# Trainium2 kernel study: moving the DRAM crossings of an encoder kernel from the ACT and POOL queues to SP's queue

## The chip, the cores and the metric

The kernel runs on one core of one Trainium2 chip. The time is device microseconds (us) of one execution. Before the change, three runs gave 878.9, 880.5 and 880.49 us, so the median is 880.49 us.

Engines are named as the profile names them: PE does the matrix multiplications, DVE and ACT work on vectors, POOL and SP here mostly issue transfers. A DMA transfer is issued by an instruction in the queue of one engine. An engine runs its queue in order, so an instruction that waits holds up everything behind it in the same queue.

## The reference

Two layers over 256 tokens of width 1024, in float32. A layer has a token mixer and a gated MLP, each with a residual:

```python
def _token_mixer(xn, w_in, w_pool, pool_scale, w_a, w_b, w_o, rel_bias):
    B, S, _ = xn.shape
    u, q, k, v, g_pool, g_attn = jnp.split(xn @ w_in, SPLITS, axis=-1)
    ...
    for gi, (window, dilation) in enumerate(ATTN_GROUPS):
        ...
        o_g, lse_g = _dilated_group(q[:, :, hs], k[:, :, hs], v[:, :, hs], bias, window, dilation)
    ...
    wts = jax.nn.softmax(jnp.stack(lses, axis=0), axis=0)
    attn = jnp.einsum('gbsh,gbshd->bshd', wts, jnp.stack(outs, axis=0).astype(jnp.float32))
    ...
    merged = jax.nn.sigmoid(g_pool) * (pool_out @ w_a) + jax.nn.sigmoid(g_attn) * (attn_out @ w_b)
    return merged @ w_o

def _conv_ffn(xn, w_up, conv_w, conv_b, w_down):
    a, gval = jnp.split(xn @ w_up, 2, axis=-1)
    a = lax.conv_general_dilated(...) + conv_b
    return (jax.nn.gelu(a) * gval) @ w_down

def reference(x, w_in, ...):
    h = x
    for layer in range(DEPTH):
        h = h + _token_mixer(_rmsnorm(h, norm1[layer]), ...)
        h = h + _conv_ffn(_rmsnorm(h, norm2[layer]), ...)
    return _rmsnorm(h, norm_f)
```

## The kernel before

**Weights.** All weights stream from DRAM once, through the class `Weights`. A load brings 1 MB into one of three `raw` buffers (L145, issued by SP; a load of the q and k weights is two issues of 512 KB). To keep the precision of float32, each load is split into two pieces, and each piece into a high part `wh` (a cast on ACT, L208) and a low part `wl` (a subtraction on DVE, L210). There are five buffers for split pieces, and PE multiplies with `wh` and `wl` in turn. `W.get()` hands out the next piece and splits the pieces that are due after it. `W.loads_behind` maps the number of a load to an instruction: that load is put into SP's queue only after this instruction (`issue_after`). It sets an order in the queue; it is not a wait for data.

**Crossings.** Some products come out of PE with tokens on the partitions and are needed with channels on the partitions. `cross` (L732) does this in three steps: two DVE transposes of 32 x 32 blocks, a write of 512 KB to a DRAM tile (L741), and four reads of 128 KB from it into a quarter of the partitions each (L746). The reads wait until the write has landed. Every layer has sixteen crossings:

- six for q and k (`n` = 0 to 5 in the loop that calls `by_tokens`, tiles "crossing" into `k` and `qk_rows`). The write is issued by ACT (`there=nc.scalar`), the reads by POOL;
- four for the probabilities, one for each head of the first group (`start_turn(hh)`, tile "turning" into `turned_p`), write on ACT, reads on POOL;
- six in the MLP (`to_z`, tile "crossing" into `zg` and `zga`), write on SP, reads on POOL.

**The stage around them.** From the q and k projections to the gates, PE, ACT and DVE run in the order in which the source is written (`manual_schedule`). The matmuls of weight pieces are `t_ps` (L692). After each piece, `step()` runs what the table `steps` has for that place: `parts` splits k and q of the first head group, `scores(hh)` (matmuls `s_ps`, L1055 and L1061, then the softmax), `start_turn(hh)`, `turn(hh)` (the high part `pth` on ACT, L1100, and the low part `ptl` on DVE, L1101) and `weigh(hh)` (matmuls `o_ps`, L1110 and L1114). `scores(0)` multiplies with k of crossing 3. `turn(0)` and `weigh(0)` come after the piece at place 28 and 29. In ACT's order the cast of the first piece of load 27 stands ahead of `pth` of `turn(0)`, and in DVE's order the subtraction of that piece stands ahead of `ptl`.

Elsewhere, the MLP among it, a scheduler orders the instructions by their dependences and by the `issue_after` that the source gives. Loads are counted within the kernel: in the first layer, loads 10 to 22 bring the weights of q and k (and one of them those inside the pooling mixer), loads 23 to 26 w_a, 27 to 30 those of the first gate, 31 to 36 those of the second gate and w_b, 37 to 40 w_o, and from load 41 on those of the MLP. `first_up[l]` has the number of the first load of w_up, 41 in the first layer; this load goes to a buffer of its own and is called by hand at place 39 of `steps`.

**Before, on SP,** nothing of the q, k and probability crossings stands in the queue. The loads follow one another as raw buffers come free. In the MLP the write of a crossing stands between loads.

Of the kernel before, what the change touches and what calls it, by code (L numbers as in the profile page):

```python
# [23 lines left out]
HPG = 4  # L24
# [73 lines left out]
class Weights:  # L98
# [8 lines left out]
    def __init__(self, tc, pool, idle):  # L107
        self.tc, self.nc, self.pool, self.idle = tc, tc.nc, pool, idle
        self.loads, self.pieces = [], []
        self.n_loaded, self.n_split, self.n_got = 0, 0, 0  # L110
        self.look = self.LOOK
        self.raw, self.split = {}, {}
        self.live = set()
        self.behind, self.later = (), []
        self.last = [None, None]
        self.loads_behind = {}
        self.n_scaled, self.gains = 0, None

    def add(self, src, shape, cuts, tag=None):
# [129 lines left out]
def encoder(ctx, tc, x, w_in, w_pool, pool_scale, w_a, w_b, w_o, norm1, norm2, w_up, conv_w,  # L249
            conv_b, w_down, rel_bias, norm_f, onehot, edges, out):  # L250
    nc = tc.nc
# [9 lines left out]
    W = Weights(tc, wpool, big)  # L261
# [32 lines left out]
    first_up = []  # L294
    for l in range(DEPTH):
# [37 lines left out]
        for f in range(4, NF, 2):  # L333
            if f in HALF_GROUPS:
                n, j = HALF_GROUPS[f]
# [343 lines left out]
    def run(gen):  # L679
        for _ in gen:  # L680
            pass

    def v_tile():
        return acc.tile([P, 512], F32, tag="acc", name="v_ps")
# [12 lines left out]
    def by_tokens(x2, n, at_once=1, then=None, ps=None, begin=0, end=None,  # L697
                  ahead=None):


        if ps is None:
            ps = [mmp.tile([P, 512], F32, tag="mm", name="t_ps") for _ in range(2)]
        for i0 in range(begin, n if end is None else end, at_once):
            if ahead:
                next(ahead)
            held = [W.get() for _ in range(at_once)]
            for t in range(2):
                for i, piece in enumerate(held, i0):
                    v_sum(ps[t], x2, t, i, piece, n - 1)
            for i, _ in held:  # L710
                W.free(i)
            if then:
                then()
        return ps

    def to_chunks(rows, y, z, parts):

        turned = nc.vector.transpose(out=y.rearrange("p q c j -> p c q j"), in_=rows)  # L720
        d = dram.tile([P, 4, P], F32, tag="turned", bufs=4, name="turned")
        nc.sync.dma_start(out=d, in_=y.rearrange("p q c j -> p q (c j)"))
        for q in range(4):
            there = nc.sync.dma_start(
                out=z[32 * q : 32 * q + 32].rearrange("p a c j -> p a (c j)"),
                in_=d[:, q].rearrange("(a i) x -> i a x", a=4),
            )
        hi, lo = (p.rearrange("p c (a j) -> p a c j", a=4) for p in parts)
        made = nc.scalar.copy(out=hi, in_=z), nc.vector.tensor_sub(out=lo, in0=z, in1=hi.bitcast(F32))
        return turned, there, made  # L730

    def cross(rows, y, z, name, after=None, there=None):  # L732

        with tc.issue_after(after.ins) if after else ExitStack():
            for t in range(2):
                nc.vector.transpose(out=y[:, t].rearrange("p q c j -> p c q j"), in_=rows[t])  # L739
        d = dram.tile([2 * P, 4, P], F32, tag=name, bufs=2, name=name)  # L740
        (there or nc.sync).dma_start(  # L741
            out=d.rearrange("(t p) q x -> p t (q x)", t=2),
            in_=y.rearrange("p t q c j -> p t (q c j)"),
        )
        for q in range(4):
            nc.gpsimd.dma_start(  # L746
                out=z[32 * q : 32 * q + 32].rearrange("p a c j -> p a (c j)"),
                in_=d[:, q].rearrange("(a i) x -> i a x", i=32),
            )

    def two_parts(tag, name):


        return big.tile([P, KD, 2, 2, P], F32R, tag=tag, name=name)
# [174 lines left out]
    for l in range(DEPTH):  # L929
# [25 lines left out]
        else:  # L955
            for g in range(NG):
                held = begun[0] if g == 0 else [W.get() for _ in range(4)]
                for t in range(2):
                    if g + t == 0:
                        ps = begun[1]  # L960
                    else:
                        ps = v_tile()
# [16 lines left out]
        for gi in range(3, -1, -1):  # L979
# [10 lines left out]
            cur, n = u, S + 2 * PAD  # L990
            sh = 1
            while sh < w:
# [3 lines left out]
                    out=nxt[:, :, 0:n], in0=cur[:, :, 0:n], in1=cur[:, :, sh : sh + n]  # L996
# [7 lines left out]
            if hw > 1:  # L1004
# [5 lines left out]
                out=pd, in0=cur[:, :, o : o + S], scalar=1.0 / w, in1=u[:, :, PAD : PAD + S],  # L1010
# [8 lines left out]
        def pool_out(po2):  # L1019
            for j in range(2):  # L1020
                i, (wh, wl) = W.get()
                for gg in range(2):
                    for oc in range(2):
                        ps = acc.tile([P, 2, S], F32, tag="acc", name="pool_ps")
                        cc = slice(oc * P, (oc + 1) * P)
                        two_sums(
                            pooled[2 * j + gg], 2,
                            (ps, lambda k: wh[:, 2 * gg + k, cc], lambda k: wl[:, 2 * gg + k, cc]),
                        )
                        c = 4 * j + 2 * gg + oc  # L1030
                        sc = hps[:, l, c : c + 1]
                        po = sm.tile([P, 2, P], F32, tag="u", name="po")
                        nc.scalar.mul(out=po, in_=halves(ps[:, 1]), mul=sc)
                        nc.vector.scalar_tensor_tensor(
                            out=po, in0=halves(ps[:, 0]), scalar=sc, in1=po, op0=ALU.mult, op1=ALU.add
                        )
                        nc.scalar.copy(out=po2[:, c, 0], in_=po)
                        nc.vector.tensor_sub(out=po2[:, c, 1], in0=po, in1=po2[:, c, 0].bitcast(F32))  # L1038
                    if gg:
                        W.free(i)  # L1040
                    yield
# [3 lines left out]
        q = big.tile([P, 2, 4, 2, P], F32, tag="q1", name="q")  # L1045
        kk = big.tile([P, 2, 2 * 4, 4, 32], F32, tag="k1", name="k")
        probs, turned, ptiles = {}, {}, {}
# [41 lines left out]
        def start_turn(hh):  # L1089
            y = sm.tile([P, 2, 4, 4, 32], F32, tag="gain", bufs=1, name="turning")  # L1090
            turned[hh] = turned_p[:, hh % 2]
            cross([probs[hh, t] for t in range(2)], y, turned[hh], "turning", there=nc.scalar)

        def turn(hh):

# [75 lines left out]
        for n in range(6):  # L1171
            block, which = divmod(n, 2)
            if n == 1:
                po2 = two_parts("m2", "po2")
            ps = by_tokens(x2, 4, then=step, ahead=pool_out(po2) if n == 1 else None)
            y = tmp[:, 1].rearrange("p (t q c j) -> p t q c j", t=2, q=4, c=4)
            if n in (2, 4):
                z = tmp[:, 0].rearrange("p (a c j) -> p a c j", a=8, c=4)
            else:

                z = kk[:, (1, 0, None, 0, None, 1)[n]]
            cross(ps, y, z, "crossing", there=nc.scalar)
            if n == 1:

                highs = big.tile([P, 2, HPG, 2, P], F32R, tag="xn", name="highs")
                qh, kh = highs[:, 0], highs[:, 1]
                lows = [
                    big.tile([P, 2, 2, 2, P], F32R, tag=f"{tag}0", name="lows") for tag in "qk"
                ]
                turned_p = big.tile([P, 2, 2 * 4, 4, 32], F32, tag="ybig", name="turned_p")  # L1190
# [4 lines left out]
        for n in range(2):  # L1195
            ps = by_tokens(po2, 4, then=step)
# [11 lines left out]
        for n in range(2):  # L1208
            th = gate("q1")
            for t in range(2):  # L1210
                nc.vector.scalar_tensor_tensor(
                    out=pa[n][:, t], in0=th[:, t], scalar=1.0, in1=pa[n][:, t],
# [11 lines left out]
        for n, cc in enumerate(HALVES):  # L1224
            th = gate("gates")
            ps = by_tokens(at2, 2, 2)
            ks = slice(4 * n, 4 * n + 4)
            y = turned_rows[:, n]
            z = big.tile([P, 2, 4, 4, 32], F32, tag=("q1", "v0")[n], name="merged")
            for t in range(2):  # L1230

                with tc.issue_after((turning if t else made[1]).ins) if n + t else ExitStack():
                    nc.vector.scalar_tensor_tensor(
                        out=th[:, t], in0=th[:, t], scalar=1.0, in1=ps[t], op0=ALU.add, op1=ALU.mult
                    )
                    nc.vector.tensor_add(out=th[:, t], in0=th[:, t], in1=pa[n][:, t])
                turning, there, made = to_chunks(
                    th[:, t], y[:, t], z[:, t], (mh[:, ks, t], ml[:, ks, t])
                )
# [43 lines left out]
        z_of = [zg[:, 0], zg[:, 1], zga[:, 0]]  # L1283
        za = zga[:, 1]

        def to_z(ps, z, after):
            y = big.tile([P, 2, 4, 4, 32], F32, tag="v0", name="crossing")
            cross(ps, y, z, "crossing", after)

        def of_chunk(z, i):  # L1290
            return z[:, :, i].rearrange("p (t a) j -> p t a j", t=2)
# [1 line left out]
        def by_halves(n):  # L1293
            ps = by_tokens(x2, 4, end=2)
            yield
            by_tokens(x2, 4, ps=ps, begin=2)
            to_z(ps, z_of[n % 3], W.last[1])
            yield

        held, ps0 = entry  # L1300
        ps1 = v_tile()
        for n in range(4):
            v_sum(ps1, x2, 1, n, held[n])
        for i, _ in held:
            W.free(i)
        to_z((ps0, ps1), za, W.behind[1])
        run(by_halves(0))

        def up(f):
# [64 lines left out]
        for n in (1, 2):  # L1374
            for j, _ in enumerate(by_halves(n)):
                up(2 * (n - 1) + j)
        groups = {n: by_halves(n) for n in range(3, NQ)}
        for f in range(4, NF, 2):
            if f in HALF_GROUPS:
# [42 lines left out]
```

## Time and profile before

| | us |
|---|---|
| median of three runs | 880.49 |
| the profiled execution | 879.22 |
| its span, first to last instruction | 877.3 |
| PE busy in it | 854.3 |
| mean granted clock of PE | 0.991 of full speed |

The span is what the profile covers; the execution is 1.9 us longer. The page of the profile lists the busy time of each engine, the span in 40 slices, the DMA queues, the chain of work that ended last, and groups of instructions. A line such as `L208 ACT CAST wh<-raw ... x274 | 283.7, 1051 | 172.7 <-PE` reads: line 208 of the kernel, on ACT, 274 instructions, 283.7 us busy, 1051 ns for one, and 172.7 us in which ACT was idle before them, mostly ended by PE. In a timeline, a row has the start, the length, engine and line, how many instructions of the same form are put together, and in brackets the idle time before them with what ended it. Two parts of the page that concern the transfers:

```profile
q1 hardware_dynamic: 112616, 171.11, 60.0%
q0 software_dynamic: 6144, 16.79, 7.1%
q10 hardware_dynamic: 5600, 10.75, 3.3%
```

These are the DMA queues with packets, megabytes and share of the time of 16 DMA engines. By their bytes, q1 is SP's (the weights), q0 POOL's (the reads of the crossings) and q10 ACT's (the writes of the q, k and probability crossings).

```profile
crossing<-qk_rows ACTq DMA_DIRECT2D x12, 512.0 KB, 6.3
crossing<-crossing SPq DMA_DIRECT2D x12, 512.0 KB, 7.3
```

These are DMA issues with their count, size and median time from issue to landing.

### The profile page before, as it was taken

To read this page: it belongs to the slowest core of one execution; us is meant where nothing else is said; L and a number is where in the kernel's file an instruction comes from. 1 tells how busy PE (TensorE), PEld (TensorE's weight loads), DVE (VectorE), ACT (ScalarE), POOL (GpSimd) and SP (SyncE) were. 2 spreads that over 40 slices of the span, in tenths; PEclk is the share of its full clock that TensorE was granted. 3 is DMA by queue.
4 is the path that set the end of the run, shared out by engine and by line. 5 is a ranking of instruction groups with operands and counts; after the bars stand their busy time and mean duration, and the time that the engine had idled before them with its cause. 6 is when DMAs were issued, how large, how long until landed. Compare 5 with 4: busy or idle time off the path is not lost. (4 is left out here: it accounts for less than half of the span.)

```text
span 877.3 us, 11562 instructions
## 1 busy us (share of the span) xinstructions
PE 854.3 (97%) x4151; PEld 721.4 (82%) x4151; DVE 663.5 (76%) x1018; ACT 486.3 (55%) x759; POOL 106.4 (12%) x226
## 2 busy tenths in 40 slices
PE   9999988999999999999999999799999999999997
PEld 7888877787888888888888888687888888888886
DVE  7997766767767888888855966577676777987884
ACT  7755542546435666666554654345554555765663
POOL 1801122220011211010000011131100122010100
PEclk9999998999999999999999999899999999999999
DMA  9686797886668878575626578869867398676641
GB/s 335 207 246 215 244 298 227 249 250 233 223 206 268 263 248 239 196 240 192 239 97 220 165 240 269 282 189 284 248 208 265 129 328 275 203 246 215 217 145 49
DMA packets 124418, 199.38 MB, mean 227 GB/s; under 512 B 6905, under 2 KB 69057, under 8 KB 124361
## 3 DMA queue, kind: packets, MB, share of 16 engines
q1 hardware_dynamic: 112616, 171.11, 60.0%
q0 software_dynamic: 6144, 16.79, 7.1%
q10 hardware_dynamic: 5600, 10.75, 3.3%
q8 instruction: 33, 0.54, 0.3%
q14 instruction: 25, 0.20, 0.1%
HBM read 178.68 MB, written 19.94 MB: 226 GB/s over the span
## 5 line engine op out<-in xcount | busy, mean ns | idle before, releaser
L210 DVE TENSOR_TENSOR wl<-raw,wh 128x1024 fp32r<-128x1024 f32 x274 | 330.5, 1221 | 124.0 <-ACT wh L208 108.0
L208 ACT CAST wh<-raw 128x1024 fp32r<-128x1024 f32 x274 | 283.7, 1051 | 172.7 <-PE t_ps L692 64.6
L692 PE MATMUL t_ps<-wh,x 128*128 128x512 f32 x960 | 302.5, 391 | 0.0
L692 PEld LDWEIGHTS t_ps<-wh,x 128*128 128x128 f32 x960 | 181.2, 189 | 37.6
L692 PE MATMUL t_ps<-wl,x 128*128 128x512 f32 x480 | 187.7, 391 | 0.0
L568 PE MATMUL proj_ps<-x,wh 128*128 128x512 f32 x448 | 106.5, 390 | 0.0
L692 PEld LDWEIGHTS t_ps<-wl,x 128*128 128x128 f32 x480 | 90.5, 189 | 18.4
L568 PEld LDWEIGHTS proj_ps<-x,wh 128*128 128x128 f32 x448 | 83.2, 188 | 16.5
L610 PE MATMUL res_ps<-wh,actq 128*128 128x512 f32 (+1 forms) x184 | 70.1, 381 | 0.0
L611 PE MATMUL res_ps<-wl,actq 128*128 128x512 f32 (+1 forms) x184 | 70.1, 381 | 0.0
L612 PE MATMUL res_ps<-wh,actk 128*128 128x512 f32 (+1 forms) x184 | 70.0, 380 | 0.0
L568 PEld LDWEIGHTS proj_ps<-x,wl 128*128 128x128 f32 x448 | 56.8, 192 | 2.2 <-DVE a L605 0.5
L568 PE MATMUL proj_ps<-x,wl 128*128 128x256 f32 x448 | 57.7, 284 | 0.0
L692 PE MATMUL t_ps<-wh,po 128*128 128x512 f32 x128 | 40.8, 393 | 0.0
L746 POOL DMA_DIRECT2D k<-crossing x32 | 18.8, 593 | 179.3 <-DVE po L1038 72.3
L612 PEld LDWEIGHTS res_ps<-wh,actk 128*128 128x128 f32 x184 | 34.6, 188 | 6.5
L610 PEld LDWEIGHTS res_ps<-wh,actq 128*128 128x128 f32 x184 | 34.6, 188 | 6.4
L611 PEld LDWEIGHTS res_ps<-wl,actq 128*128 128x128 f32 x184 | 34.6, 188 | 6.3
L746 POOL DMA_DIRECT2D zg<-crossing x32 | 18.4, 583 | 171.8 <-DVE y L1325 49.1
L1077 ACT ACTIVATE p<-s,nm 128x512 f32<-128x512 f32 x16 | 11.6, 724 | 36.2 <-DVE nm L1074 34.2
L477 POOL TENSOR_SCALAR ss<-ss 128x1 f32<-128x1 f32 x8 | 1.8, 222 | 226.9 <-ACT junk L470 226.9
L1321 ACT ACTIVATE y<-a,prm 128x256 f32<-128x256 f32 x44 | 25.4, 598 | 6.1 <-DVE a L605 5.2
(204 smaller groups left out, 1212.6 us busy)
## 6 DMA issues: line engine op xcount, KB each, us to landing
raw<-in_w_up_dram SPq DMA_DIRECT2D x44, 1024.0 KB, 6.4
raw<-in_w_in_dram SPq DMA_DIRECT2D x34, 1024.0 KB, 7.5
raw<-in_w_in_dram SPq DMA_DIRECT2D x50, 512.0 KB, 5.4
raw<-in_w_down_dram SPq DMA_DIRECT2D x22, 1024.0 KB, 4.9
raw<-in_w_a_dram SPq DMA_DIRECT2D x8, 1024.0 KB, 11.2
raw<-in_w_o_dram SPq DMA_DIRECT2D x8, 1024.0 KB, 5.8
crossing<-qk_rows ACTq DMA_DIRECT2D x12, 512.0 KB, 6.3
crossing<-crossing SPq DMA_DIRECT2D x12, 512.0 KB, 7.3
```

Source lines behind the costliest of these rows:

```text
L208: inst = nc.scalar.copy(out=h, in_=src)
L210: inst = nc.vector.tensor_sub(out=l, in0=src, in1=h.bitcast(F32))
L477: nc.gpsimd.tensor_scalar_add(ss[:, 3:4], ss[:, 0:1], EPS)
L568: nc.tensor.matmul(out, w(k), x, start=(steps is first and k == 0), stop=(steps is last and k == nk - 1), skip_group_check=turns["rest"],)
L610: nc.tensor.matmul(ps, ah, wh, start=first, stop=False, skip_group_check=on)
L611: nc.tensor.matmul(ps, ah, wl, start=False, stop=False, skip_group_check=on)
L612: nc.tensor.matmul(ps, al, wh, start=False, stop=last, skip_group_check=on)
L692: nc.tensor.matmul(ps, x2[:, 2 * n + j, part, t, :], w[:, j, :], start=(n + m == 0), stop=(n == last and m == 5),)
L746: nc.gpsimd.dma_start(out=z[32 * q : 32 * q + 32].rearrange("p a c j -> p a (c j)"), in_=d[:, q].rearrange("(a i) x -> i a x", i=32),)
L1077: nc.scalar.activation(p, s, AF.Exp, bias=nm[:, 0:1], accum_out=z)
L1321: nc.scalar.activation(y, a, AF.Identity, bias=b, scale=w1)
```

## The change

`cross` issues the write and the four reads on SP, in all three uses. A write is put into SP's queue after the last read of the crossing before it (`W.there`), so that crossings do not interleave. The load that is next to be issued (`but=0`), the one after it (`but=1`, for the first q and k crossing) or the third (`but=2`, for the crossing into `za` in the MLP) is put behind the last read. The load that `first_up` names is put behind the reads of the fourth turning. The arguments `there=nc.scalar` go, and `to_z` and `cross` get `but`. What is computed stays the same, and so does the order of PE, ACT and DVE in the source.

The order of SP's queue in the first layer is then: half of load 16, the write of crossing 0, the other half, its reads, loads 17 and 18, write 1, reads 1, loads 19 and 20, write 2, reads 2, loads 21 and 22, write 3, reads 3, loads 23 and 24, write 4, reads 4, load 25, write and reads of turning 0, load 26, write 5, reads 5, load 27, turning 1, loads 28 and 29, turning 2, loads 30 and 31, turning 3, loads 32 to 34, load 41, load 35.

```diff
--- before.py
+++ after.py
@@ -113,7 +113,7 @@
         self.live = set()
         self.behind, self.later = (), []
         self.last = [None, None]
-        self.loads_behind = {}
+        self.loads_behind, self.there = {}, None
         self.n_scaled, self.gains = 0, None
 
     def add(self, src, shape, cuts, tag=None):
@@ -729,7 +729,7 @@
         made = nc.scalar.copy(out=hi, in_=z), nc.vector.tensor_sub(out=lo, in0=z, in1=hi.bitcast(F32))
         return turned, there, made
 
-    def cross(rows, y, z, name, after=None, there=None):
+    def cross(rows, y, z, name, but=0, after=None):
 
 
 
@@ -738,15 +738,19 @@
             for t in range(2):
                 nc.vector.transpose(out=y[:, t].rearrange("p q c j -> p c q j"), in_=rows[t])
         d = dram.tile([2 * P, 4, P], F32, tag=name, bufs=2, name=name)
-        (there or nc.sync).dma_start(
-            out=d.rearrange("(t p) q x -> p t (q x)", t=2),
-            in_=y.rearrange("p t q c j -> p t (q c j)"),
-        )
+
+        with tc.issue_after(W.there.ins) if W.there else ExitStack():
+            nc.sync.dma_start(
+                out=d.rearrange("(t p) q x -> p t (q x)", t=2),
+                in_=y.rearrange("p t q c j -> p t (q c j)"),
+            )
         for q in range(4):
-            nc.gpsimd.dma_start(
+            there = nc.sync.dma_start(
                 out=z[32 * q : 32 * q + 32].rearrange("p a c j -> p a (c j)"),
                 in_=d[:, q].rearrange("(a i) x -> i a x", i=32),
             )
+        W.loads_behind[W.n_loaded + but] = W.there = there
+        return there
 
     def two_parts(tag, name):
 
@@ -1089,7 +1093,9 @@
         def start_turn(hh):
             y = sm.tile([P, 2, 4, 4, 32], F32, tag="gain", bufs=1, name="turning")
             turned[hh] = turned_p[:, hh % 2]
-            cross([probs[hh, t] for t in range(2)], y, turned[hh], "turning", there=nc.scalar)
+            there = cross([probs[hh, t] for t in range(2)], y, turned[hh], "turning")
+            if hh == HPG - 1:
+                W.loads_behind[first_up[l][1]] = there
 
         def turn(hh):
 
@@ -1179,7 +1185,7 @@
             else:
 
                 z = kk[:, (1, 0, None, 0, None, 1)[n]]
-            cross(ps, y, z, "crossing", there=nc.scalar)
+            cross(ps, y, z, "crossing", int(n == 0))
             if n == 1:
 
                 highs = big.tile([P, 2, HPG, 2, P], F32R, tag="xn", name="highs")
@@ -1283,9 +1289,9 @@
         z_of = [zg[:, 0], zg[:, 1], zga[:, 0]]
         za = zga[:, 1]
 
-        def to_z(ps, z, after):
+        def to_z(ps, z, but, after):
             y = big.tile([P, 2, 4, 4, 32], F32, tag="v0", name="crossing")
-            cross(ps, y, z, "crossing", after)
+            cross(ps, y, z, "crossing", but, after)
 
         def of_chunk(z, i):
             return z[:, :, i].rearrange("p (t a) j -> p t a j", t=2)
@@ -1294,7 +1300,7 @@
             ps = by_tokens(x2, 4, end=2)
             yield
             by_tokens(x2, 4, ps=ps, begin=2)
-            to_z(ps, z_of[n % 3], W.last[1])
+            to_z(ps, z_of[n % 3], 0, W.last[1])
             yield
 
         held, ps0 = entry
@@ -1303,7 +1309,7 @@
             v_sum(ps1, x2, 1, n, held[n])
         for i, _ in held:
             W.free(i)
-        to_z((ps0, ps1), za, W.behind[1])
+        to_z((ps0, ps1), za, 2, W.behind[1])
         run(by_halves(0))
 
         def up(f):
```

## The prediction

> **What bounds the kernel now.** I read the page's busy times first, then what each wait of PE cost, then PE's timeline where the waits are, then the queues that feed those places.
>
> ```profile
> span 877.3 us, 11562 instructions
> PE 854.3 (97%) x4151; PEld 721.4 (82%) x4151; DVE 663.5 (76%) x1018; ACT 486.3 (55%) x759; POOL 106.4 (12%) x226
> ```
>
> PE is busy for 854.3 of 877.3 us, so nothing that leaves its instructions alone can win more than the 23 us in which it is idle, apart from its clock.
>
> ```profile
> PE s_ps L1061 <- DMA k<-crossing: 11.3, 2, 6.2
> PE o_ps L1110 <- DVE ptl L1101: 3.3, 4, 1.0
> PE o_ps L1110 <- ACT pth L1100: 1.4, 2, 0.8
> ```
>
> In the list of waits (total, times, longest) 16 us lie at two places of the attention stage, once in each layer: 11.3 before the scores, where a crossing of k is late, and 4.7 before the weighing.
>
> ```profile
> 128.50 0.28 PE L1055 MATMUL s_ps<-highs,lows 128*128 128x256 f32 x1
> 133.85 1.20 PE L1061 MATMUL s_ps<-k,q 128*128 128x128 f32 x4 [5.08 <-DMA k<-crossing]
> ...
> 136.19 0.77 PE L692 MATMUL t_ps<-wh,x 128*128 128x512 f32 x1
> 136.77 0.63 PE L692 MATMUL t_ps<-wl,x 128*128 128x512 f32 x1
> 137.19 0.83 PE L692 MATMUL t_ps<-wh,x 128*128 128x512 f32 x2
> ...
> 145.49 0.61 PE L1061 MATMUL s_ps<-k,q 128*128 128x128 f32 x4
> ...
> 146.66 0.48 PE L692 MATMUL t_ps<-wh,po 128*128 128x512 f32 x1
> ...
> 561.05 0.28 PE L1055 MATMUL s_ps<-highs,lows 128*128 128x256 f32 x1
> 567.52 1.19 PE L1061 MATMUL s_ps<-k,q 128*128 128x128 f32 x4 [6.19 <-DMA k<-crossing]
> ```
>
> The stall has a tail. The eleven matmuls behind it start over 2.34 us (133.85 to 136.19); the same eleven undisturbed take 1.17 (145.49 to 146.66), and the next two t_ps take 1.00 where 0.46 is usual. With what follows I put the tail at 1.9 us. [...]
>
> ```profile
> 161.36 0.38 PE L1110 MATMUL o_ps<-pth,vh 128*128 128x256 f32 x1 [0.81 <-ACT pth L1100]
> 162.70 0.39 PE L1110 MATMUL o_ps<-ptl,vh 128*128 128x256 f32 x1 [0.96 <-DVE ptl L1101]
> 162.93 0.28 PE L1110 MATMUL o_ps<-pth,vl 128*128 128x256 f32 x1
> ...
> 200.60 0.39 PE L1110 MATMUL o_ps<-ptl,vh 128*128 128x256 f32 x1 [0.96 <-DVE ptl L1101]
> ...
> 596.09 0.39 PE L1110 MATMUL o_ps<-ptl,vh 128*128 128x256 f32 x1 [0.96 <-DVE ptl L1101]
> ...
> 633.33 0.39 PE L1110 MATMUL o_ps<-ptl,vh 128*128 128x256 f32 x1 [0.45 <-DVE ptl L1101]
> ```
>
> The gaps at the first weighing are short, and the matmul behind them keeps its 0.23 us spacing (162.70 to 162.93): no tail. The crossing that is late runs like this in the queues:
>
> ```profile
> 102.85 2.30 POOL L746 DMA_DIRECT2D k<-crossing  x4 [18.14 <-DMA crossing<-qk_rows]
> 114.00 2.30 POOL L746 DMA_DIRECT2D qk_rows<-crossing  x4 [8.84 <-DMA crossing<-qk_rows]
> 123.97 2.30 POOL L746 DMA_DIRECT2D k<-crossing  x4 [7.68 <-DMA crossing<-qk_rows]
> ```
>
> ```profile
> 95.25 14.83 SPq L145 DMA_DIRECT2D raw<-in_w_in_dram  x8
> 116.44 13.64 SPq L145 DMA_DIRECT2D raw<-in_w_a_dram  x4
> 144.76 19.42 SPq L145 DMA_DIRECT2D raw<-in_w_in_dram  x4
> ```
>
> The reads of crossing 3 (counted from 0) are issued by POOL at 123.97 and land at 133.7, beside loads that SP issues with no regard to them from 116.44 on.
>
> **The change part by part.** Nothing is computed otherwise. ACT loses 20 writes (0.37 us of issue each) and POOL 128 reads (0.58 each). ACT sat idle before most of its casts and POOL has 12% of the span busy, so both count for nothing; without that cover ACT would win 20 times 0.37, 7 us.
>
> SP takes all of it: per crossing one write and four reads. Each waits on SP for what it needs, and the next load stands behind. So from the second crossing on, SP's queue is one chain of links: four reads are issued, a load (or two) is issued, the next write goes out behind the load, it lands, and only then the next reads go. PE's own work no longer sets when raw27 is loaded; this chain does. A link has no row of its own. Its parts have:
>
> ```profile
> 267.42 0.37 SPq L145 DMA_DIRECT2D raw<-in_w_up_dram  x1
> 270.31 0.37 SPq L741 DMA_DIRECT2D crossing<-crossing  x1
> ...
> 284.63 6.16 SPq L145 DMA_DIRECT2D raw<-in_w_up_dram  x2
> 291.64 0.37 SPq L741 DMA_DIRECT2D crossing<-crossing  x1
> ```
>
> ```profile
> 274.87 2.40 POOL L746 DMA_DIRECT2D zga<-crossing  x4 [15.84 <-DMA crossing<-crossing]
> ...
> 300.02 2.30 POOL L746 DMA_DIRECT2D zg<-crossing  x4 [10.64 <-DMA crossing<-crossing]
> ```
>
> ```profile
> 217.09 0.34 SPq L722 DMA_DIRECT2D turned<-turned  x1
> 219.09 1.77 SPq L724 DMA_DIRECT2D merged<-turned  x4
> ```
>
> In the MLP a write already follows a load on SP. From the load's issue to the first read it was 7.45 us (267.42 to 274.87) with the engines otherwise quiet, and 9.6 (290.42, the end of the row of two less 0.37, to 300.02) beside other reads. POOL may wake later than SP would, so I take 7.2 for the clean case. The four reads then take SP 1.8 (1.77 in the row of merges). A link with one load is 9.0; its bounds are 3.8, if the write need not wait for the load (2.0 from write to next read in the row of 217.09, and 1.8), and 11.4 (9.6 and 1.8). I stay near the quiet row, since no reads of POOL run any more, though the reads are still in flight when the load starts.
>
> [...]
>
> ```profile
> DMA packets 3370, 3.41 MB, mean 341 GB/s; under 512 B 51, under 2 KB 3369, under 8 KB 3369
> ```
>
> This is the DMA view of 35 to 45 us, where q and k weights come back to back: 1.05 MB at 341 GB/s is 3.1 us, the price of the second load in a link that has two.
>
> ```profile
> L741 ACTq DMA_DIRECT2D crossing<-qk_rows x1: 372/372/372, 96.5 to 96.5; - x1
> ```
>
> The chain starts when crossing 1's rows are ready, at 96.5, set by PE and the transposes. Nothing is ahead of that write, so it takes 2.7 (2.0 for half the bytes in the row of 217.09, up to the 6.4 of 96.5 to 102.85), and its reads 1.8: raw19 is issued at 101.0. Three links of two loads (9.0 and 3.1) bring raw21 to 113.1, raw23 to 125.2, raw25 to 137.3; two of one load bring raw26 to 146.3 and raw27 to 155.3. Before, raw27 was issued at 144.76. The two ends of a link put it at 129 (the chain then sets nothing and the old 144.76 stays) and at 167.
>
> What this does to PE. Crossing 3's reads are issued by 125.2 and land some 2 us later, at 127, ahead of PE's 128.6: the stall before the scores goes, with its tail. PE then comes to the first weighing at about 160.16 − 5.1 − 1.9 = 153. In the hand-written order, the first of raw27's two casts stands ahead of pth on ACT, and the first subtraction ahead of ptl on DVE:
>
> ```profile
> 159.74 1.05 ACT L208 CAST wh<-raw 128x1024 fp32r<-128x1024 f32 x1
> 160.69 0.62 ACT L1100 CAST pth<-turned_p 128x512 fp32r<-128x512 f32 x1
> ```
>
> ```profile
> raw<-in_w_in_dram SPq DMA_DIRECT2D x50, 512.0 KB, 5.4
> ```
>
> So the load is late next. With 5.4 us from issue to landing, raw27 is there at 160.7. From the cast's start (159.74) to the o_ps that needs ptl (162.70) it is 2.96 us, so PE resumes at 163.6, 0.9 later than before. In the second layer everything is 432.55 later (561.05 less 128.50): 596.15 against 596.09, 0.1 later. Each of these stalls is now some 9 us of idle in one piece, so the tail of 1.9 comes with it, twice: 3.8. What is won behind it: the crossings of turned probabilities and the loads after raw27 come closer together, and the stalls at the last weighing (0.96 and 0.45) go: −1.4.
>
> In the MLP the write was on SP; four reads per crossing come to it and hold loads by up to 6 us. What covers that are the five split pieces that PE has ahead of it, some 2.7 us of matmuls each:
>
> ```profile
> L208 ACT CAST wh<-raw 128x1024 fp32r<-128x1024 f32 x274 | 283.7, 1051 | 172.7 <-PE t_ps L692 64.6
> ```
>
> The casts wait most often for PE to free a piece, not for a load, so I cost the MLP at nothing; without this cover it is the third rival. The first load of w_up is held behind the fourth turning; its use lies beyond the weighing, and it also costs nothing.
>
> The sum: 0.9 + 0.1 + 3.8 − 1.4 = +3.4 us. On the profiled execution (879.2 us, its span 877.3) that is 882.6; the median shown is 1.3 above that execution, so 883.9 to be compared with 880.5.
>
> **The rivals.** First, the link is shorter than 9.0 and the stall goes without a successor: faster. Each 0.1 us of link moves raw27 by 0.5, in two layers 1.0 in all, so the forecast is no change at about 8.7. [...] With the chain no limit at all, both stalls and the tail go: 11.3 + 4.7 + 3.8 = 19.8, 861. For it: the 16 us of wait are real, and the reads no longer fight with loads. Against it: a write behind a load never showed less than 7.45.
>
> Second, a link is as long as the contended 9.6 shows, 11.4 with the reads: five links 2.4 longer are 12 a layer, and 24 is 907; halfway, 895. [...] Against it: that row had POOL's reads beside it.
>
> Third, the MLP starves. Between 267 and 312 us ten loads of 2.6 to 3.1 and four crossings that add 5.9 each (9.0 less 3.1) ask for some 52 us of a 45 us stretch: 7 late a layer. PE's pieces ahead cover 13. If half of that is not there when the first crossing starts, some 7 a layer are lost: 897. That SP waits mostly for split pieces to come free speaks against it.
>
> That the change doesn't do what it says is no rival: in the order in which the changed kernel's instructions stand, all writes and reads are on SP, each with its loads behind it.
>
> **How the numbers follow.** The forecast has 0.45, the first rival 0.33, the second 0.12, the third 0.10. The likeliest time is 883.9. About 0.2% (1.8 us) can be told from no change in a measurement of this kernel. The forecast's own range, links of 8.5 to 9.5, is 879 to 889, so of its 0.45 some 0.10 lies within 0.2% and 0.05 below: faster 0.38, same 0.10, slower 0.52. The range reaches halfway into the first rival, 866, and past the middle of the second and third, 899.
>
> **What would show it.** On PE, no wait of s_ps for k, and one long wait of o_ps for pth at the first weighing, with matmuls at half speed behind it; the clock in the slices there stays under 1. On SP, raw27 issued near 155 and each write's landing about 7 us after the load ahead of it. It is wrong if raw27 is issued before 150 (the link is shorter, faster), if s_ps still waits, or if PE waits for wl in the MLP.

## The result and the profile after

The changed kernel takes 886.92 us (median of 10 runs, 881.73 to 888.92), the kernel before 880.27 (10 runs, 878.9 to 884.23). The ratio is 1.0065, with a 95% interval of 1.0044 to 1.0085: slower by 6.6 us, where +3.4 was forecast. The profiled execution took 887.31 us, 8.1 more than the one shown of before. Its page begins:

```profile
span 884.8 us, 11537 instructions
PE 854.9 (97%) x4151; PEld 722.1 (82%) x4151; DVE 662.0 (75%) x1018; ACT 485.2 (55%) x759; POOL 32.2 (4%) x98
```

PE has the same busy time within 0.6 us, and the span is 7.5 longer, so PE is idle for longer. Its waits, in total, times and longest:

```profile
PE o_ps L1116 <- ACT pth L1106: 18.7, 2, 10.3
PE t_ps L692 <- DVE wl L210: 2.2, 2, 1.6
PE o_ps L1116 <- DVE ptl L1107: 1.5, 2, 0.8
...
PE s_ps L1065 <- DMA k<-crossing: 0.7, 1, 0.7
```

The 11.3 us before the scores have become 0.7. In their place stand 18.7 us at the first weighing, in each layer one wait. PE's timeline has them, with the idle time and its releaser in brackets:

```profile
128.65 0.61 PE L1065 MATMUL s_ps<-k,q 128*128 128x128 f32 x4
...
164.69 0.58 PE L1116 MATMUL o_ps<-pth,vh 128*128 128x256 f32 x1 [10.29 <-ACT pth L1106]
166.03 0.58 PE L1116 MATMUL o_ps<-ptl,vh 128*128 128x256 f32 x1 [0.76 <-DVE ptl L1107]
166.41 0.41 PE L1116 MATMUL o_ps<-pth,vl 128*128 128x256 f32 x1
...
601.36 0.58 PE L1116 MATMUL o_ps<-pth,vh 128*128 128x256 f32 x1 [8.39 <-ACT pth L1106]
602.70 0.58 PE L1116 MATMUL o_ps<-ptl,vh 128*128 128x256 f32 x1 [0.76 <-DVE ptl L1107]
```

PE passes the scores 5.2 us earlier than before (128.65 against 133.85), and goes on after the first weighing 3.3 later (166.03 against 162.70). The matmul behind the wait keeps 0.38 us of distance instead of 0.23 (162.70 to 162.93 before), and from 164.6 to 168.4 the granted clock of PE is 0.50. ACT's timeline says what `pth` stood behind:

```profile
163.07 1.04 ACT L208 CAST wh<-raw 128x1024 fp32r<-128x1024 f32 x1 [6.22 <-DMA raw<-in_w_in_dram]
164.02 0.61 ACT L1106 CAST pth<-turned_p 128x512 fp32r<-128x512 f32 x1
```

ACT waited 6.2 us for a load of weights, cast its first piece, and only then made `pth`. That load is 27, and SP's timeline has the chain that leads to it (L743 writes, L748 reads, L145 loads):

```profile
95.46 0.37 SPq L743 DMA_DIRECT2D crossing<-qk_rows  x1
98.50 1.81 SPq L748 DMA_DIRECT2D k<-crossing  x4
100.42 2.04 SPq L145 DMA_DIRECT2D raw<-in_w_in_dram  x4
...
112.53 2.08 SPq L145 DMA_DIRECT2D raw<-in_w_in_dram  x4
114.70 0.65 SPq L743 DMA_DIRECT2D crossing<-qk_rows  x1
123.61 1.81 SPq L748 DMA_DIRECT2D k<-crossing  x4
125.51 0.95 SPq L145 DMA_DIRECT2D raw<-in_w_a_dram  x2
...
145.77 0.40 SPq L145 DMA_DIRECT2D raw<-in_w_a_dram  x1
146.26 0.45 SPq L743 DMA_DIRECT2D crossing<-qk_rows  x1
155.21 1.80 SPq L748 DMA_DIRECT2D k<-crossing  x4
157.11 0.40 SPq L145 DMA_DIRECT2D raw<-in_w_in_dram  x1
```

Read it as links: a load or two, the next write right behind, a gap until that write has landed (the reads go out 8.9 us behind the write at 114.70 and 9.0 behind the one at 146.26), the reads, the next load. The rows left out are of the same kinds; nothing else stands in this queue for 60 us, and the gaps are most of it.

### The profile page after: what moved, and what is told of

Read it like the earlier page. It is cut to its first block, busy times and chain, and to the rows that moved or that the text cites. A ratio compares the mean times of both kernels' runs of the same rounds, so it can differ in the third digit from the quotient of the medians.

```text
span 884.8 us, 11537 instructions
## 1 busy us (share of the span) xinstructions
PE 854.9 (97%) x4151; PEld 722.1 (82%) x4151; DVE 662.0 (75%) x1018; ACT 485.2 (55%) x759; POOL 32.2 (4%) x98
## 4 chain that ended last, share of the span: by engine, by line
PE 87%; DMA 7%; DVE 3%; SPq 1%; issue 1%; ACT 1%; POOLq 0%; POOL 0%; ACTq 0%; DVEq 0%
PE t_ps L692 35%; PE proj_ps L568 18%; PE v_ps L692 6%; PE res_ps L610 6%; PE res_ps L611 6%; PE res_ps L612 6%; DMA crossing<-qk_rows 4%; PE v_ps L925 2%; DMA turning<-turning 2%; DVE wl L210 1%; PE v_ps L832 1%; DMA raw<-in_w_a_dram 1%; PE o_ps L1120 1%; PE pool_ps L568 1%; PE o_ps L1116 1%
## 5 line engine op out<-in xcount | busy, mean ns | idle before, releaser
L692 PEld LDWEIGHTS t_ps<-wh,po 128*128 128x128 f32 x128 | 24.0, 188 | 5.6 <-ACT wh L208 0.8
L1361 ACT CAST actq<-g 128x256 fp32r<-128x256 f32 x44 | 17.0, 403 | 20.6 <-DVE g L1350 20.0
L692 PE MATMUL t_ps<-wl,po 128*128 128x512 f32 x64 | 25.2, 393 | 2.2 <-DVE wl L210 2.2
L470 ACT ACTIVATE junk<-h 128x512 f32<-128x512 f32 (+1 forms) x19 | 10.5, 554 | 29.4 <-DVE h L468 29.3
```

Source lines behind the costliest of these rows:

```text
L470: nc.scalar.activation(junk[:, 0 : cc.stop - cc.start], h[:, t, cc], AF.Square, scale=D**-0.5, accum_out=ss[:, n : n + 1],)
L692: nc.tensor.matmul(ps, x2[:, 2 * n + j, part, t, :], w[:, j, :], start=(n + m == 0), stop=(n == last and m == 5),)
L1361: nc.scalar.copy(out=ah, in_=g)
```

## The experiments

The theory was that the holds make SP's queue a chain which delivers load 27 late, and that PE's first weighing stands behind that load in ACT's and DVE's order. The rivals were the MLP, the crossings of the probabilities themselves, and the transfers as such. All times are medians, and each ratio is to runs of the kernel before that were taken beside it; these had medians of 879.0 (first four), 879.34 (next four) and 879.89 (last three).

**Which stage.** The first kernel keeps the change in the attention stage alone, the second in the MLP alone:

```diff
 # e1_qk_only: the MLP's crossings as before
+        if mlp:
+            nc.sync.dma_start(out=d..., in_=y...)
+            for q in range(4):
+                nc.gpsimd.dma_start(out=z..., in_=d[:, q]...)
+            return
```

```diff
 # e2_mlp_only: the q, k and probability crossings as before
+        if there:
+            there.dma_start(out=d..., in_=y...)
+            for q in range(4):
+                nc.gpsimd.dma_start(out=z..., in_=d[:, q]...)
+            return
```

> The attention stage as in the changed kernel, the six MLP crossings as before (write on SP, reads on POOL, no load held). Theory (the loss is the late raw27 before the first weighing): the loss stays, about 887 us (+6 to +7 on the kernel before). Rival (the loss is made in the MLP, where SP's queue is nearly full): it falls back to about 880 us.

> The MLP crossings as in the changed kernel, the attention stage as before (writes on ACT, reads on POOL, no load held). Theory: no change that can be measured, 879 to 881 us, no wait of PE in the MLP. Rival (MLP): about 886 us.

The attention stage alone takes 886.59 us, ratio 1.0083 (1.0056 to 1.0111); the MLP alone takes 878.74, ratio 0.9982 (0.9957 to 1.0008). Both are as expected. The whole loss is in the attention stage; the MLP's part cannot be told from nothing. In the profile of the first, the long wait is there again:

```profile
PE o_ps L1127 <- ACT pth L1117: 16.9, 2, 9.2
```

The same link that took 11.3 us in the execution shown above (145.77 to 157.11) took 8.9 here (145.99 to 154.93), with the same attention stage: from one execution to another such a link can differ by 2 us.

**Where PE waits.** One number is altered, in the changed kernel and in the kernel before:

```diff
-            28: ((turn, 0),),
+            27: ((turn, 0),),
```

> The changed kernel with one number altered: turn(0) at place 27 of the table instead of 28, so that on ACT and DVE the first probabilities are split ahead of the first piece of load 27 and PE's first weighing no longer stands behind that load. Queues and holds stay. Theory: raw27 is still issued near 157 us, but PE's wait of 10.3 us at o_ps goes; PE then waits some 3 us for k of crossing 5, landed at 159, and the time falls by about 8 us a layer, to about 871. Rival (the weighing waits for the crossing of the probabilities itself, not for the load): the wait stays where it is, 887.

> The kernel before with the same one number altered. Theory: the 16 us stay at the scores' side (11.3), only the waits of the first weighing go, some 2 us a layer: about 876. If the order of the split is what gains by itself, whatever the queues are, it would fall as far as the changed kernel does (-16).

The changed kernel takes 877.25 us with it, ratio 0.9977 (0.9958 to 0.9995), about 10 less than without. The kernel before takes 876.45, ratio 0.996 (0.9937 to 0.9983), as expected; its wait for k stays:

```profile
PE s_ps L1061 <- DMA k<-crossing: 12.5, 3, 6.7
```

In the changed kernel with the new place, load 27 is nearly as late as without (155.58 against 157.11), but `pth` no longer stands behind it:

```profile
153.98 0.61 ACT L1106 CAST pth<-turned_p 128x512 fp32r<-128x512 f32 x1
```

```profile
PE o_ps L1116 <- ACT pth L1106: 5.9, 3, 3.2
PE o_ps L1116 <- DVE ptl L1107: 4.4, 4, 1.1
```

So the wait was for the load, not for the crossing of the probabilities. The gain was expected to be 16 and is 10: PE did not wait for k, as I had it, but came to the second weighing some 15 us behind the first (first `o_ps` at 154.80, then 3.2 us of wait until 172.78), and the `pth` of that one stands behind the casts of load 28, held behind the second turning. The chain has a next load for every order that is mended by one place.

**The hold.** These kernels leave the crossings on SP and alter what is held:

```diff
 # e5_behind_write: the load goes behind the write
-        W.loads_behind[W.n_loaded + but] = W.there = there
+        W.loads_behind[W.n_loaded + but] = wrote
+        W.there = there
 # and the first load of w_up is not held
```

```diff
 # e6_hold3: held behind the reads of crossings 0 to 3 alone
+        if hold:
+            W.loads_behind[W.n_loaded + but] = there
+        W.there = there
-            cross(ps, y, z, "crossing", int(n == 0))
+            cross(ps, y, z, "crossing", int(n == 0), hold=n < 4)
 # turnings: hold=False; the first load of w_up stays held
```

```diff
 # e7_nohold
-        W.loads_behind[W.n_loaded + but] = W.there = there
+        W.there = there
 # and the first load of w_up is not held
```

```diff
 # e9_early27: in the changed kernel only the load behind crossing 5 is moved
+        W.loads_behind[W.n_loaded + but] = wrote if early else there
+            cross(ps, y, z, "crossing", int(n == 0), early=n == 5)
```

> As the changed kernel, but the next load stands behind the crossing's write instead of behind its reads (and the first load of w_up is not held): the order on SP is write, load, reads, so that the load fills the time in which the write lands. Theory (the chain of links write-behind-load sets raw27): raw27 is issued at about 147 us, right behind crossing 5's write, instead of 157; both stalls are gone, 861 to 867. Rival (the transfers themselves are the limit, the engines have no room for what SP now carries): raw27 still lands after 160, about 885.

> As the changed kernel, but loads are held only behind crossings 0 to 3 of q and k (and in the MLP), no longer behind 4, 5 and the four turnings. Theory: crossing 3's reads go out near 124 as now, so the stall at the scores stays away; from there on loads go out behind writes and raw27 is issued at about 147: 862 to 868. Rival (the hold behind the first four crossings is what costs, since it starts the chain late): raw27 past 152, 875 to 885.

> As the changed kernel with no load held anywhere; crossings on SP in the same order. Theory: like the kernel with the load behind the write, 861 to 868. If holding loads is what keeps crossing 3 early, the wait of s_ps for k comes back with some 5 us a layer and the time is 872 to 880.

> The changed kernel with one load moved in each layer: load 27 stands behind the write of crossing 5 instead of behind its reads. All other holds stay. Theory: raw27 is issued near 147 us instead of 157, its 10 us of wait at o_ps shrink to what loads 26 and the crossings before it leave, 0 to 2 us, and the time is 866 to 872. Rival (several loads are late together, and the next of them takes the stall over): 878 to 885.

| | us | ratio to before | interval |
|---|---|---|---|
| load behind the write (e5) | 856.96 | 0.9769 | 0.9725 to 0.9813 |
| no load held (e7) | 857.32 | 0.9773 | 0.9736 to 0.981 |
| held behind crossings 0 to 3 (e6) | 870.44 | 0.9913 | 0.9886 to 0.9939 |
| load 27 alone behind a write (e9) | 876.72 | 0.9973 | 0.9945 to 1.0002 |

The first two beat both kernels, by 22 us the one before and by 30 the changed one, and lie 4 us below what was expected. e6 missed its expected range by 2.4 us, and e9 came out between the ranges of its theory and its rival. The page of e5 and its SP timeline:

```profile
span 855.2 us, 11536 instructions
PE 848.4 (99%) x4151; PEld 718.3 (84%) x4151; DVE 664.0 (78%) x1018; ACT 487.1 (57%) x759; POOL 32.0 (4%) x98
```

```profile
113.00 0.37 SPq L743 DMA_DIRECT2D crossing<-qk_rows  x1
113.47 0.42 SPq L145 DMA_DIRECT2D raw<-in_w_a_dram  x1
117.97 1.81 SPq L748 DMA_DIRECT2D k<-crossing  x4
...
139.99 0.40 SPq L743 DMA_DIRECT2D crossing<-qk_rows  x1
140.49 0.41 SPq L145 DMA_DIRECT2D raw<-in_w_in_dram  x1
```

Now a load goes out 0.5 us behind the write (113.47 and 113.00), and the reads follow 5.0 us behind the write, against 8.9 in the changed kernel. Crossing 3's reads go out at 118.0, 5.6 us earlier than with the hold, and load 27 at 140.5, 17 earlier. PE has no wait of the attention stage left. Against the kernel before, PE's idle time falls from 23.0 us (877.3 less 854.3) to 6.8 (855.2 less 848.4), and its busy time by 5.9, with a granted clock of 0.998 instead of 0.991. The hold therefore did the opposite of helping the crossing: a load that leaves behind the reads is in front of the next write.

Load 27 alone was expected to bring 15 to 20 us and brought 10. It was issued at 147.13, ten earlier than in the changed kernel, but:

```profile
156.81 1.04 ACT L208 CAST wh<-raw 128x1024 fp32r<-128x1024 f32 x1 [1.61 <-DMA raw<-in_w_in_dram]
```

Its cast started only 6.3 us earlier (156.81 against 163.07): it was issued right behind load 26 (146.09) and a write (146.58), and needed 9.7 us to be there. The lateness is in the whole chain, not in its last load. That also shows in e6, where the queue up to the reads of crossing 3 is as in the changed kernel (123.79 against 123.61) and 3.6 us of wait stay at the first weighing of the second layer. DVE's timeline has the same delay at another place, first in the changed kernel, then in e5:

```profile
134.09 0.69 DVE L1072 SCALAR_TENSOR_TENSOR s<-s_ps,bt 128x512 f32<-128x512 f32 x1
```

```profile
129.28 0.69 DVE L1073 SCALAR_TENSOR_TENSOR s<-s_ps,bt 128x512 f32<-128x512 f32 x1 [1.21 <-PE s_ps L1066]
```

PE's first scores are ready at about the same time in both (128.65 and 128.63 for their last group's start), but in the changed kernel DVE takes them 4.8 us later, since two subtractions, whose casts waited 6.4 us for a load of w_a, stand ahead of them in its order (131.81, idle 4.8 us before).

**The queues.** Three kernels ask what the move to SP's queue itself is worth, two with the writes and one with the reads elsewhere:

```diff
 # e8_act_writes: writes of the attention stage on ACT, the holds stay
 # e11_act_writes_nohold: the same, and no load held
-            nc.sync.dma_start(out=d...)
+            (by or nc.sync).dma_start(out=d...)     # by=nc.scalar
```

```diff
 # e10_pool_reads: as e5, but the reads of the attention stage on POOL
-            there = nc.sync.dma_start(out=z...)
+            there = (nc.gpsimd if pool else nc.sync).dma_start(out=z...)
```

> As the changed kernel, but the writes of the attention stage go back to ACT's queue; reads and held loads stay on SP. [...] Rival (bandwidth, not order, sets the link): raw27 at 156 to 158 as now, about 887.

> In the attention stage the writes on ACT as before, the reads on SP, no load held anywhere. Theory (ACT's queue stands still at each write until DVE's transposes are done, some 2.4 us, and casts behind it are late): the s_ps wait is gone or below 3 us, but short waits of t_ps or o_ps for casts stay, 862 to 872. Rival (the engine that issues the writes is of no account): 857 as with the writes on SP.

> In the attention stage the writes on SP with the next load behind the write, but the reads on POOL's queue as in the kernel before; the MLP with the load behind the write. Tells whether SP's reads are needed for what the kernel with the load behind the write gained (857). Theory (what counts is that no load is put ahead of a write that is ready, and that ACT no longer waits for the transposes): 857 to 864, no s_ps wait above 2 us. Rival (reads on POOL's queue lose against loads, as before the change): an s_ps wait of 4 to 6 us a layer, 868 to 876.

With the reads on POOL it takes 859.35 us, ratio 0.9778 (0.9745 to 0.981), 2.4 more than with them on SP, as expected. Set beside the kernel before, which also has them on POOL, the write of crossing 3 goes out at 113.14 instead of 117.67 and its reads at 118.58 instead of 123.97. So the reads need not be on SP: the writes on SP, with the next load behind each, bring nearly all of the gain.

With the writes on ACT it takes 881.36, ratio 1.003 (0.9997 to 1.0064), with the holds (e8), and 876.05, ratio 0.9962 (0.9931 to 0.9993), without (e11). Both miss what I had estimated, 868 to 876 for e8 and 862 to 872 for e11. In e8 load 27 is issued at 151.01, within the 149 to 152 of my estimate, and PE's waits at the first weighing fall from 20.2 us in all to 3.7. But PE now waits for casts, for 7.7 us where the changed kernel has 0.3:

```profile
PE t_ps L692 <- ACT wh L208: 7.7, 2, 4.2
```

The longest of these is for one cast, of which e8 has the first row and the changed kernel the second:

```profile
153.71 1.04 ACT L208 CAST wh<-raw 128x1024 fp32r<-128x1024 f32 x1 [2.37 <-DVE turning L739]
```

```profile
148.40 1.04 ACT L208 CAST wh<-raw 128x1024 fp32r<-128x1024 f32 x1
```

It starts 5.3 us later. ACT stands still for 2.4 us until DVE's transposes are done, issues the write of turning 1, and only then makes this cast. The cast before it had already come 2.8 later (145.47 against 142.64), behind the write of crossing 5. The first softmax, ahead of both, is at the same place in the two kernels (135.43 and 135.53). So what makes this cast late is ACT's standing at the writes.

e11 is 19 us slower than e7 (857.32), and the edit between them is again the engine of the writes alone. But these 19 us are not ACT's standing alone, since the order on SP changes with it. In e7, load 23 leaves at 113.23, behind the write of crossing 3 and ahead of its reads (117.69), and load 27 at 140.21. In e11 no write stands on SP, and the loads come behind the reads again, as with the hold:

```profile
123.36 1.93 SPq L748 DMA_DIRECT2D k<-crossing  x4
125.34 1.00 SPq L145 DMA_DIRECT2D raw<-in_w_a_dram  x2
...
151.74 0.40 SPq L145 DMA_DIRECT2D raw<-in_w_in_dram  x1
```

The waits of e11 are:

```profile
PE t_ps L692 <- ACT wh L208: 9.0, 3, 4.2
PE t_ps L692 <- DVE wl L210: 2.3, 3, 0.8
PE s_ps L1065 <- DMA k<-crossing: 1.7, 1, 1.7
```

The cast for which PE waits longest starts at 154.17 in e11, at 148.40 in the changed kernel and at 142.58 in e7. Of the 11.6 us between e11 and e7, half is there with the writes on SP too, behind late loads. How the 19 us of time divide between the two causes no run shows.

Whether a write lands earlier beside a load than behind it stays open. The last link of e8 is short because the write of crossing 5 goes out on ACT ahead of load 26 (144.71 and 145.16; its reads at 149.13). Behind loads, the time from the loads to the reads was 9.4 us in e8 and 11.1 in the changed kernel at crossing 3 (113.66 to 123.08; 112.53 to 123.61), and 9.8 in both at crossing 4. These two crossings do not settle it.

## Why the prediction was right, and where its sizes were off

**The stall before the scores goes.** Right: 0.7 us are left, in the second layer.

**SP's queue is one chain and sets load 27.** Right, and shown by e5 and e7, in which the chain is gone and so is the wait. Loads 19, 21, 23, 25 and 26 were issued at 100.4, 112.5, 125.5, 137.2 and 145.8; forecast were 101.0, 113.1, 125.2, 137.3 and 146.3. The last link was put at 9.0 and took 11.3 in the profiled execution, 8.9 in e1: a size that varies. Load 27 came at 157.1 instead of 155.3, and needed 6.0 us to its cast (163.07) instead of 5.4.

**The first weighing waits for load 27.** Right, shown by e3. By its size, +0.9 and +0.1 were forecast and +3.3 and +3.1 measured (166.03 against 162.70; 602.70 against 596.09, less the 3.5 by which PE reaches the scores of layer 1 later, 564.56 against 561.05). This is the term that was mis-sized. In layer 0, 1.8 of the 2.4 missing are the last link, 0.6 the landing. In layer 1 the links of two loads took 12.8 to 14.2 us, forecast was 12.1; PE also waited 1.9 us just before (the waits of `t_ps`), which the forecast did not have, but that wait shortened the one behind it by as much. That the landing came out near its 5.4 us is luck: the row it was read from holds issues of 512 KB, and load 27 is one issue of 1 MB, for which the page of before has

```profile
raw<-in_w_in_dram SPq DMA_DIRECT2D x34, 1024.0 KB, 7.5
```

Measured were 6.0 and 6.1 us to the cast.

**The slow matmuls behind the wait.** 1.9 each were forecast; PE fell back by a further 1.7 in layer 0 and 1.8 in layer 1, as the second weighing shows (180.77 against 175.73; 617.57 against 609.11). The granted clock of PE was 0.50 from 164.6 to 168.4, behind 10.3 us of idle, and in the kernel before 0.50 from 133.8 to 137.4, behind 5.1 us. The end of the range at 866 rests on an estimate that a stall of some 3 us would leave hardly such a tail, which no run shows: behind a wait of 3.7 us in e9 (ended at 158.43) the matmuls of the first weighing had 0.37 us of distance (159.77 to 160.14), against 0.23 in the kernel before.

**The last weighing.** −1.4 was forecast for both layers together. Matched matmul by matmul, PE is 5.0 and 8.5 us behind the kernel before ahead of it, and 3.6 and 7.8 behind it: −1.4 and −0.7, with −0.1 and −0.2 more over the rest of each layer. The two waits are gone. But in layer 0 of the changed kernel the last weighing stands behind 19 more matmuls `t_ps` in PE's order (its first `o_ps` at 208.57, 199.25 before), so the reason that was given, crossings and loads closer together, is not shown.

**The sum.** Forecast 0.9 + 0.1 + 3.8 − 1.4 = +3.4. Measured 3.3 + 3.1 + 1.7 + 1.8 − 1.5 − 0.9 = +7.5, by which the span grew. The execution profiled is 0.4 us above the median. The mechanism was forecast, and its size was half of what came. The totals of the slower rivals (907, 895, 897) were counted from 882.6 and not from 883.9, so they are 1.3 too low.

**The MLP costs nothing.** Right (e2: 0.9982, with 1 in its interval).

**ACT's queue gains nothing by losing the writes.** This step was wrong, though it is no term of the sum. I priced the issues (0.37 us each) and not the wait that each of them has in ACT's order, with casts behind it. The waits of ACT in the kernel before had it (total, times, longest):

```profile
ACT wh L208 <- DVE qk_rows L739: 26.8, 8, 3.8
ACT wh L208 <- DVE turning L739: 13.1, 5, 3.0
```

In the changed kernel the gain does not show, since PE waits for load 27 at the first weighing whether its casts were early or not. e8 shows it: 7.7 us of PE's waits for casts against 0.3.

**The rival that ends faster** (no stall takes the place of the one removed, 861) is what e5 and e7 are, at 857. Its condition, a link of clearly less than 8.7 us, was not met by the changed kernel, in which a load stands ahead of each write.

## What to carry to other kernels

When a transfer in two steps (a write, then reads that wait for it) shares a queue with a stream of loads, let the next load go out between the two steps: here that took 856.96 us (e5), while with the load behind the reads, where it stands ahead of the next write and makes a chain of the whole queue, it took 886.92. Before a wait is mended, ask which instruction stands next in the same order on the engine that was waiting; here the late load only moved from one consumer to the next until the chain itself was opened. And price an instruction in an engine's queue by how long it stands there waiting (up to 3.8 us for a write on ACT here), not by how long its issue takes (0.37).

## What the runs showed of the hardware that was not expected

- The kernels with stalls scattered more. The kernel before ranged over 875.8 to 886.2 us in one series of 19 runs and the changed one over 7 us in 10, but e5 and e7, which have no stall of this stage left, stayed within 0.4 us (856.75 to 857.16) and 0.9 us (856.78 to 857.71), in only four runs each. Why is not shown.
- A load that was issued 10 us earlier was ready only 6.3 us earlier (e9); a load and a write had been issued within the 1.1 us ahead of it, in the same queue.
- The engine that issues the reads mattered little (2.4 us, e10 against e5). A write on ACT held ACT for up to 3.8 us until the transposes were done, and the casts behind it with it (the kernel before; e8 against the changed kernel).
